# Strassen-Winograd block pairs of weights: the first block sum as A22 + A21, summed by a load and an accumulating DMA, where it was A21 − A22 over a copy of A22 that GpSimd negates

## The chip, the cores and the metric

The kernel runs on one core of one Trainium2 chip. A core has a matrix engine (TensorE, PE in the profile; its weight loads are listed apart as PEld), VectorE (DVE), ScalarE (ACT), GpSimd (POOL) and SyncE (SP, which here only issues DMAs), and 16 DMA engines that move data between the memory of the chip (HBM) and the core's on-chip memory. Matrix products land in PSUM. The metric is the time of one execution on the device, in microseconds (us).

## What is computed

Two layers of a small diffusion transformer over 256 latent tokens and 256 context tokens, width 1024, all in fp32. Each layer has a gated feed-forward network (FFN, hidden width 2816), a mixer, and a second FFN; layer 0 mixes by a short convolution, layer 1 by attention. Cut to what matters here:

```python
def _swiglu(h, w13, w2):
    gte, up = jnp.split(h @ w13, 2, axis=-1)
    return (jax.nn.silu(gte) * up) @ w2

def _short_conv_mixer(h, w_in, k, w_out):
    bgate, cgate, xv = jnp.split(h @ w_in, 3, axis=-1)
    return (bgate * _dwconv3(cgate * xv, k)) @ w_out
```

The FFNs run on latent and context tokens together (512 columns), except the last one, which runs on the latent tokens alone.

## The kernel before

**Tiling.** Activations are held transposed: features on the 128 partitions, tokens along the free dimension. An fp32 product is made of three matmuls: every operand is split into a high and a low part (`split`, L106: ScalarE rounds the high part, L107; VectorE subtracts to get the low part, L108), and `mm3` (L132) adds high·high (L136), high·low (L137) and low·high (L138) in PSUM.

**Block pairs.** Two tiles of 128 output features (gate and up of one hidden tile, for instance) times two halves of the contraction (512 features each) times two halves of the tokens (latent and context) make a 2×2 by 2×2 block product. The class `Pair` (L697 to L787) computes it by the Strassen-Winograd scheme: seven block products of 12 matmuls each (128×128 weights, 256 tokens) where the plain way needs eight. It needs sums of the weight blocks, S1 to S4, and sums of the activation blocks, T1 to T4. The T sums are made once for an input (`Blocks.sums`, L407, and `FirstBlocks.sums`, L443), the S sums for every pair. There are 66 pairs: 56 in the FFNs (first matrix `w13`) and 10 in the convolution mixer (`cw_cx`, `cw_b`). The first tiles of a stage (two, or six in the first FFN) are computed the plain way (`opening`, L789, the first steps of the kernel and L830), while the blocks are still being normalised.

**How one pair gets its weights.** In HBM a pair's weights are one row of 2048 columns for each partition, as four blocks of 512 columns: A21, A11, A22, A12. `Pair.__init__` (L704) fills two raw tiles of 1024 columns, r1 and r2, from a pool of eight such buffers (tag `wr`):

- SP loads r2 = [A22 | A12], 512 KB (`load_raw`, L103).
- SP loads A11 into the right half of r1, 256 KB (L708).
- POOL writes −A22 into the left half of r1 (L710), which needs r2 landed and r1's buffer free.
- POOL issues a DMA that adds A21 from HBM onto it (L713): S1 = A21 − A22.
- A11 and A12 are split for the products that use them as they are (L718).

`sums(0)` then has VectorE turn A11 into S2 = A11 − S1 in place (L732), and r1 as a whole, S1 beside S2, is split in one go (L733, by L107 and L108). `sums(1)` splits A22 into tiles of their own, w4h and w4l: ScalarE makes the high part and its negative (L112, L113), and a DMA issued by POOL adds A22 from HBM again (L114). Then VectorE subtracts S2 from both halves of r2 (L740: S3 = A22 − S2, S4 = A12 − S2), and r2 is split.

**Order of the products.** `head` (A11, A12), `five` (S1·T1, the first to need S1; its matmuls write q and read th, tl), `six` (S2·T2, S4·B22), then `seven` (S3·T3) and `four` (A22·T4) of the pair before. Between them ScalarE copies partial sums out of PSUM (L757, L763, L767) and VectorE adds and multiplies the results (L769, L777, L786).

**What sets the order.** Each engine and each queue runs its instructions in one fixed order and waits on semaphores. That order is laid out when the program is built, by a planner with modelled costs of instructions, except where the code holds it by hand (`manual_schedule`: the first steps and the attention heads) or ties one instruction behind another (`issue_after`). POOL's queue carries, beside L710 and L713, the A22 accumulations (L114) and those that add an FFN's output to x (L567), all in one line. Other users of the `wr` buffers are the second FFN matrices (`w2a`, `w2b`) and the rows of the modulation matrix (`modT`), which VectorE reduces in the gaps (L177). An FFN goes in three parts, each a run of pairs and then a projection by `w2`; the first pairs of the next part are loaded during the projection.

## Time and profile before

| quantity | value |
| --- | --- |
| runs of the kernel | 1545.27, 1545.4, 1546.8 us; median 1545.4 us |
| the profiled execution: its time | 1545.56 us |
| the profiled execution: span from first to last instruction | 1543.8 us |
| busy time PEld, DVE, ACT, POOL | 1423.8, 1299.2, 850.3, 301.3 us |
| granted TensorE clock, whole span | 1.000 |
| moved by DMA | 278.80 MB, mean 181 GB/s; 262.07 MB read from HBM |

The profile is of one execution, so terms are compared with its own span; its time is 1.8 us above its span and 0.16 us above the median of the runs. A line of the timeline reads: start in us from the first instruction, duration in us, engine, line of the code, operation, tile written <- tiles read, shapes, count, and in brackets the idle time of the engine before it with what ended it. A line of the windows reads: stretch, its length, then for each engine its busy time and count of instructions, the granted clock, the mean busy share of the 16 DMA engines, and GB/s.

### The profile page before, as it was taken

How to read it: one execution, taken by the hardware profiler on the slowest of the kernel's cores; microseconds unless marked ns; L12 is line 12 of the kernel's file. 1: busy time of each engine (PE TensorE's matmuls, PEld its weight loads, DVE VectorE, ACT ScalarE, POOL GpSimd, SP SyncE). 2: the span in 40 equal slices, each digit the busy share in tenths (PEclk: the TensorE clock that was granted, in tenths of full speed). 3: DMA queues.
4: the chain of work that ended last, by engine and by line, in shares of the span. 5: the costliest groups of instructions: out<-in, count | busy, mean ns of one | idle time of the engine just before them, and what ended most of it. 6: DMA issues, size and time to landing. Idle time of an engine off the chain costs nothing.

```text
span 1543.8 us, 27341 instructions
## 1 busy us (share of the span) xinstructions
PE 1532.5 (99%) x10594; PEld 1423.8 (92%) x10594; DVE 1299.2 (84%) x1970; ACT 850.3 (55%) x1474; POOL 301.3 (20%) x265
## 2 busy tenths in 40 slices
PE   9999999999999999999999999999999999999999
PEld 6898998999999899999899899989899899998888
DVE  5888788898999999978979889958868788897676
ACT  5644554645665376446456476446456456774553
POOL 0003313402231022042152102142052002300000
PEclk9999999999999999999999999999999999999999
DMA  9568768775356646686796625786697743476562
GB/s 380 198 191 232 161 186 227 170 193 143 76 144 181 201 104 142 216 208 150 209 212 149 213 72 127 222 184 149 212 218 175 257 156 112 150 244 219 169 195 76
DMA packets 97474, 278.80 MB, mean 181 GB/s; under 512 B 11456, under 2 KB 13120, under 8 KB 97344
## 3 DMA queue, kind: packets, MB, share of 16 engines
q1 hardware_dynamic: 69408, 228.10, 45.9%
q0 software_dynamic: 25920, 47.20, 18.3%
q10 hardware_dynamic: 2016, 1.76, 0.4%
q8 instruction: 83, 1.36, 0.4%
q14 instruction: 47, 0.39, 0.1%
HBM read 262.07 MB, written 1.05 MB: 170 GB/s over the span
## 4 chain that ended last, share of the span: by engine, by line
PE 93%; DVE 4%; ACT 1%; DMA 1%; issue 1%; POOL 0%; SPq 0%; DVEq 0%; ACTq 0%; POOLq 0%
PE py L137 9%; PE py L136 9%; PE py L138 9%; PE p L138 8%; PE p L137 8%; PE p L136 8%; PE q L138 6%; PE q L136 6%; PE q L137 6%; PE py L144 2%; PE pu L144 2%; PE pg L144 2%; PE py L146 1%; DVE wl L108 1%; PE pg L146 1%; PE pu L146 1%
## 5 line engine op out<-in xcount | busy, mean ns | idle before, releaser
L107 ACT ACTIVATE wh<-wr 128x1024 fp32r<-128x1024 f32 (+2 forms) x454 | 401.2, 909 | 303.9 <-PE py L137 96.2
L108 DVE TENSOR_TENSOR wl<-wr,wh 128x1024 fp32r<-128x1024 f32 (+2 forms) x454 | 469.8, 1057 | 105.5 <-ACT wh L107 83.8
L177 DVE CUSTOM_DVE_ANT_0 junk<-wr,scbc,first 128x1024 bf16<-128x1024 f32 x209 | 270.4, 1294 | 2.2 <-DMA wr<-in_modT 0.2
L137 PE MATMUL py<-gl,wh 128*128 128x512 f32 (+1 forms) x570 | 213.4, 374 | 0.0
L136 PE MATMUL py<-gh,wh 128*128 128x512 f32 (+1 forms) x570 | 213.4, 374 | 0.0
L138 PE MATMUL py<-gh,wl 128*128 128x512 f32 (+1 forms) x570 | 212.8, 373 | 0.0
L710 POOL TENSOR_SCALAR wr<-wr 128x512 f32<-128x512 f32 x66 | 125.9, 1907 | 423.2 <-DMA wr<-in_w 182.3
L137 PE MATMUL p<-tl,wh 128*128 128x256 f32 x528 | 149.4, 283 | 0.0
L138 PE MATMUL p<-th,wl 128*128 128x256 f32 x528 | 149.4, 283 | 0.0
L136 PE MATMUL p<-th,wh 128*128 128x256 f32 x528 | 149.4, 283 | 0.0
L138 PEld LDWEIGHTS py<-gh,wl 128*128 128x128 f32 x570 | 107.3, 188 | 19.2
L136 PEld LDWEIGHTS py<-gh,wh 128*128 128x128 f32 x570 | 107.4, 188 | 18.3
L137 PEld LDWEIGHTS py<-gl,wh 128*128 128x128 f32 x570 | 107.4, 189 | 18.0
L138 PE MATMUL q<-bh,wl 128*128 128x256 f32 x400 | 113.2, 283 | 0.0
L137 PE MATMUL q<-bl,wh 128*128 128x256 f32 x400 | 113.2, 283 | 0.0
L136 PE MATMUL q<-bh,wh 128*128 128x256 f32 x400 | 113.2, 283 | 0.0
L137 PEld LDWEIGHTS p<-tl,wh 128*128 128x128 f32 x528 | 101.3, 192 | 0.4
L136 PEld LDWEIGHTS p<-th,wh 128*128 128x128 f32 x528 | 101.3, 192 | 0.4
L138 PEld LDWEIGHTS p<-th,wl 128*128 128x128 f32 x528 | 101.3, 192 | 0.0
L114 POOL DMA_DIRECT2D w4l<-in_w x56 | 52.8, 944 | 231.9 <-ACT w4l L113 174.6
L567 POOL DMA_DIRECT2D x<-yg x48 | 45.3, 1008 | 213.5 <-ACT yg L564 172.7
L740 DVE TENSOR_TENSOR wr<-wr,wr 128x1024 f32<-128x1024 f32 x66 | 81.5, 1235 | 1.8 <-ACT w4h L112 0.2
(321 smaller groups left out, 4154.1 us busy)
## 6 DMA issues: line engine op xcount, KB each, us to landing
wr<-in_w SPq DMA_DIRECT2D x120, 512.0 KB, 5.0
wr<-in_modT SPq DMA_DIRECT2D x113, 512.0 KB, 5.1
wr<-in_w2b SPq DMA_DIRECT2D x64, 448.0 KB, 3.9
wr<-in_w2a SPq DMA_DIRECT2D x32, 512.0 KB, 4.6
wr<-in_w SPq DMA_DIRECT2D x56, 256.0 KB, 4.3
wr<-in_w POOLq DMA_DIRECT2D x56, 256.0 KB, 6.0
w4l<-in_w POOLq DMA_DIRECT2D x56, 256.0 KB, 5.6
x<-yg POOLq DMA_DIRECT2D x48, 256.0 KB, 7.8
```

What stands on the lines that cost most here:

```text
L107: nc.scalar.activation(out=hi, in_=src, func=AF.Copy)
L108: return nc.vector.tensor_tensor(out=lo, in0=src, in1=hi.bitcast(F32), op=ALU.subtract)
L114: nc.gpsimd.dma_start(out=lo, in_=src, accum_op=ALU.add)
L136: nc.tensor.matmul(ps, wh, mh, start=first, stop=False, **kw)
L137: nc.tensor.matmul(ps, wh, ml, start=False, stop=False, **kw)
L138: return nc.tensor.matmul(ps, wl, mh, start=False, stop=last, **kw).ins
L144: nc.tensor.matmul(ps, w[0], m[2], start=first and n == 0, stop=False)
L146: nc.tensor.matmul(ps[:, :S], w[1], m[0], start=False, stop=last and n == len(ms) - 1)
L177: nc.vector.tensor_tensor_reduce(out=junk, in0=raw, in1=scbc[:, v, :], scale=0.5 if ch in (2, 8) else 1.0, scalar=modb[:, l, col : col + 1 ...
L567: nc.gpsimd.dma_start(out=x[:, m, :], in_=t, accum_op=ALU.add)
L710: nc.gpsimd.tensor_scalar(out=r1[:, :T2], in0=r2[:, :T2], scalar1=-1.0, scalar2=None, op0=ALU.mult)
L740: tt(out=v(r2), in0=v(r2), in1=s2.unsqueeze(1).to_broadcast([P, 2, T2]), op=ALU.subtract,)
```

## The change

`Pair` and the T sums take the other signs of the scheme: S1 = A22 + A21, S2 = S1 − A11, T3 = B22 − B12, T2 = B22 − T1; S3, S4, T1 and T4 keep their forms. r1 becomes [A11 | A22] by one load of 512 KB, as the two blocks lie side by side in HBM, and POOL's DMA adds A21 onto the right half. POOL's negated copy is gone, A22 is read from HBM twice by plain loads (into r1 and r2), and S2 and S1 swap places in r1.

```diff
             elif n == 1:
-                tt(out=b12, in0=b22, in1=b12, op=ALU.add)
-                tt(out=b22, in0=b22, in1=b11, op=ALU.add)
+                tt(out=b12, in0=b22, in1=b12, op=ALU.subtract)
+                tt(out=b22, in0=b22, in1=b11, op=ALU.subtract)
                 keep("T2", b22)
...
             for q in range(2):
-                tt(out=b(0, 1, q), in0=b(1, 1, q), in1=b(0, 1, q), op=ALU.add)
-                tt(out=b(1, 1, q), in0=b(1, 1, q), in1=b(0, 0, q), op=ALU.add)
+                tt(out=b(0, 1, q), in0=b(1, 1, q), in1=b(0, 1, q), op=ALU.subtract)
+                tt(out=b(1, 1, q), in0=b(1, 1, q), in1=b(0, 0, q), op=ALU.subtract)
                 keep("T2", q, b(1, 1, q))
...
             r2 = load_raw(src[:, 1024:2048])
             r1 = wp.tile([P, 1024], F32, name=nm("wr"), tag="wr", bufs=8)
-            nc.sync.dma_start(r1[:, T2:], src[:, T2:1024])
-
-            nc.gpsimd.tensor_scalar(
-                out=r1[:, :T2], in0=r2[:, :T2], scalar1=-1.0, scalar2=None, op0=ALU.mult
-            )
-            nc.gpsimd.dma_start(out=r1[:, :T2], in_=src[:, :T2], accum_op=ALU.add)
+            nc.sync.dma_start(r1, src[:, T2 : T2 + 1024])
+
+            nc.gpsimd.dma_start(out=r1[:, T2:], in_=src[:, :T2], accum_op=ALU.add)
             self.raw = [r1, r2]
             ts = half()
             for i, key in enumerate(("A11", "A12")):
                 self.w[key] = [t[:, i * T2 : i * T2 + T2] for t in ts]
-                split(*self.w[key], self.raw[i][:, T2:])
+                split(*self.w[key], self.raw[i][:, i * T2 : i * T2 + T2])
...
             r1, r2 = self.raw
-            s1, s2 = r1[:, :T2], r1[:, T2:]
+            s1, s2 = r1[:, T2:], r1[:, :T2]
             tt = nc.vector.tensor_tensor
             if n == 0:
-                tt(out=s2, in0=s2, in1=s1, op=ALU.subtract)
-                self.keep(("S1", "S2"), r1)
+                tt(out=s2, in0=s1, in1=s2, op=ALU.subtract)
+                self.keep(("S2", "S1"), r1)
                 return
```

## The prediction

> **What bounds the kernel now.** I read the page first, then TensorE's waits, then single stretches.

> ```profile
> span 1543.8 us, 27341 instructions
> ...
> PE 1532.5 (99%) x10594; PEld 1423.8 (92%) x10594; DVE 1299.2 (84%) x1970; ACT 850.3 (55%) x1474; POOL 301.3 (20%) x265
> ...
> q1 hardware_dynamic: 69408, 228.10, 45.9%
> ...
> PE 93%; DVE 4%; ACT 1%; DMA 1%; issue 1%; POOL 0%; SPq 0%; DVEq 0%; ACTq 0%; POOLq 0%
> ```

> TensorE is busy 99% of the span and holds 93% of the chain that ended last; POOL, whose work the change takes away, holds 0% of it. A busy TensorE need not be at its full rate, so I looked at the count of matmuls in stretches of pure pair work:

> ```profile
> 800.00:820.00 20.00, 20.00 (x169) 20.00 (x168) 17.74 (x26) 12.68 (x22) 7.49 (x7) 1.00 0.60 129
> 1160.00:1180.00 20.00, 20.00 (x169) 20.00 (x168) 17.52 (x23) 12.65 (x23) 6.62 (x6) 1.00 0.80 182
> 260.00:280.00 20.00, 18.69 (x136) 17.64 (x135) 16.51 (x22) 10.55 (x19) 11.22 (x11) 1.00 0.98 225
> ```

> 169 matmuls in 20 us, 118 ns each, at a DMA share of 0.60 and at 0.80 alike: there TensorE runs at its own pace and neither loads nor POOL slow it. The third row is another kind of place, the start of a part of an FFN, where pairs and projection meet: the 16 DMA engines are full (0.98) and TensorE loses 1.3 us. All its waits between 60 and 1200 us, where all pairs lie:

> ```profile
> PE pg L136 <- ACT bh L391: 1.4, 1, 1.4
> PE q L136 <- ACT gm L763: 1.3, 1, 1.3
> PE p L138 <- DVE wl L108: 0.6, 1, 0.6
> PE pg L137 <- DVE bl L392: 0.2, 1, 0.2
> ```

> These are 3.5 us. That is the most that any relief of the other engines can visibly bring; beyond it only the 118 ns could shrink, and the change takes away no matmul.

> **The change part by part. 1, the signs.** Subtractions take the place of additions and S1 swaps sides with S2. Both operations are there now, at the same shape:

> ```profile
> L769 DVE TENSOR_TENSOR sg<-q,sg 128x512 f32<-128x512 f32 x66 | 45.3, 686 | 4.0 <-PE q L138 1.8 <-ACT wh L107 1.1 <-issue 0.5
> L732 DVE TENSOR_TENSOR wr<-wr 128x512 f32<-128x512 f32 x66 | 45.2, 685 | 9.8 <-DMA wr<-in_w 9.6
> L710 POOL TENSOR_SCALAR wr<-wr 128x512 f32<-128x512 f32 x66 | 125.9, 1907 | 423.2 <-DMA wr<-in_w 182.3 <-DVE wl L108 134.7 <-ACT wh L107 35.4
> ```

> The addition (L769) takes 686 ns, the subtraction (L732) 685: cost 0.

> **2, the negated copy.** 66 copies of 1907 ns leave POOL: 125.9 us. On the chain of POOL that is nothing, as it holds 0%. They may also hold up VectorE while they run. Two places show it:

> ```profile
> 257.76 2.09 POOL L710 TENSOR_SCALAR wr<-wr 128x512 f32<-128x512 f32 x1
> 258.04 1.48 DVE L108 TENSOR_TENSOR wl<-wr,wh 128x512 fp32r<-128x512 f32 x1
> ```
> ```profile
> 407.43 2.36 DVE L108 TENSOR_TENSOR tl<-hr,th 128x1024 fp32r<-128x1024 f32 x2
> 407.61 3.52 POOL L710 TENSOR_SCALAR wr<-wr 128x512 f32<-128x512 f32 x1 [22.03 <-DVE wl L108]
> ```

> At 258 us a subtraction of 128x512 takes 1.48 us beside a copy, where L732 takes 0.69: 0.79 us lost in a copy of 2.09, a share of 0.38, which over 125.9 us would be 48 us of VectorE time. At 407 us it is POOL that loses (3.52 instead of 1.91 us), and two subtractions take 1.18 us each. So VectorE gets back between 0 and 48 us of its 1299.2. TensorE sees of that only what it waits for VectorE, 0.6 + 0.2 us; the 0.6 follows right behind the copy at 407 us, where VectorE wasn't slowed, so I take 0 there and keep −0.8 as the bound. At 258 us VectorE idles soon after (below): 0.

> [...]

> **3, the larger load.** 66 times 256 KB more on SP's queue are 17.3 MB. That queue's 228.10 MB took 45.9% of 1543.8 us, 3.1 us for each MB, so the addition is 54 us of DMA time, 0.81 us in each pair of 9.9 us (84 matmuls of 118 ns); a share of 0.80 becomes 0.88. How much later r1 lands:

> ```profile
> wr<-in_w SPq DMA_DIRECT2D x120, 512.0 KB, 5.0
> ...
> wr<-in_w SPq DMA_DIRECT2D x56, 256.0 KB, 4.3
> ```

> 0.7 us between the medians. At worst, where the engines are full, 262 kB at 225 GB/s are 1.2 us; at best 0, if the bytes go beside the others. I take 0.7 in steady stretches, as the medians come mostly from there, and 1.2 at starts.

> **4, what S1 waits for.** Now L713 follows the copy, which needs r2 landed and r1's buffer free. After, it needs r1's own load landed. A steady pair, with the landing of the load issued at 1154.31 and of the accumulation issued at 1156.84 below it:

> ```profile
> 1154.02 0.87 POOL L114 DMA_DIRECT2D w4l<-in_w  x1 [7.14 <-ACT w4l L113]
> 1154.31 0.33 SPq L708 DMA_DIRECT2D wr<-in_w  x1
> 1154.59 1.84 POOL L710 TENSOR_SCALAR wr<-wr 128x512 f32<-128x512 f32 x1
> 1156.84 0.91 POOL L713 DMA_DIRECT2D wr<-in_w  x1 [0.41 <-POOL wr L710]
> 1167.84 0.68 DVE L732 TENSOR_TENSOR wr<-wr 128x512 f32<-128x512 f32 x1
> 1171.20 0.28 PE L138 MATMUL p<-th,w4l 128*128 128x256 f32 x1
> ```
> ```profile
> DMA to landing us min/median/max: 3.4/3.4/3.4
> ```
> ```profile
> DMA to landing us min/median/max: 6.3/6.3/6.3
> ```

> Now S1 lands at 1156.84 + 6.3 = 1163.1 and VectorE uses it at 1167.84: a lead of 4.7 us. After: 1154.31 + 3.4 + 0.7 for the load, 0.4 for the handover to POOL as in the bracket of L713, so L713 starts at 1158.8 instead of 1156.84 and S1 lands at 1165.1. The lead falls to 2.7 us; cost 0. Waiting behind L713 in POOL's line are accumulations of A22 (L114) and of x. The one issued at 1154.02 is used first at 1171.20, 17 us on; 2 us of delay cost nothing there. Without the lead, VectorE would wait in L732, and everything behind it with it.

> **5, the starts of the parts.** There is no lead:

> ```profile
>   DMA wr<-in_w: 9.6, 6
> ```
> ```profile
> 256.47 0.92 POOL L713 DMA_DIRECT2D wr<-in_w  x1 [0.41 <-POOL wr L710]
> 261.92 0.69 DVE L732 TENSOR_TENSOR wr<-wr 128x512 f32<-128x512 f32 x1 [1.19 <-DMA wr<-in_w]
> 266.07 3.75 DVE L108 TENSOR_TENSOR wl<-wr,wh 128x1024 fp32r<-128x1024 f32 x3
> 267.65 0.28 PE L136 MATMUL q<-th,wh 128*128 128x256 f32 x1
> 270.63 1.06 ACT L107 ACTIVATE wh<-wr 128x1024 fp32r<-128x1024 f32 x1 [1.77 <-PE p L137]
> ```
> ```profile
> 782.28 0.69 DVE L732 TENSOR_TENSOR wr<-wr 128x512 f32<-128x512 f32 x1 [1.68 <-DMA wr<-in_w]
> 784.22 2.83 DVE L108 TENSOR_TENSOR wl<-wr,wh 128x1024 fp32r<-128x1024 f32 x2
> 789.85 0.28 PE L136 MATMUL q<-th,wh 128*128 128x256 f32 x1
> ```
> ```profile
> DMA to landing us min/median/max: 8.4/8.4/8.4
> ```

> In 6 of the 66 pairs VectorE stood at L732 until S1 landed (first row, from the line's own waits), 9.6 us together. In the pair of L713 at 256.47 the load into r1 had been issued at 247.0 and took 8.4 (the last row), to 255.4. After: 255.4 + 1.2 + 0.4 = 257.0 instead of 256.47, so S1 comes 0.5 us later, and up to 1.7 if the accumulation loses another 1.2 in the full queues. The low half of S1 is ready at 266.07 + 3.75/3 = 267.3 and TensorE takes it at 267.65: a lead of 0.3. TensorE's loss there is 0.2 to 1.4 us; I take **0.5**, near the lower end, because removing the copy also removes the 0.79 that VectorE lost at 258. At 782 us the low half is ready at 784.22 + 1.4 = 785.6 and wanted at 789.85: 4.2 us of lead hide such a delay. The loss of 1.3 us at 271 (TensorE waiting for L763) has ScalarE's order as its cause: L763 stands behind the L107 of 270.63, which itself waits for TensorE. The change doesn't touch that: 0.

> **The sum**: 0 + 0 + 0 + 0 + 0.5 = +0.5 us on the profiled execution's 1545.56, 1546.1; that execution lies 0.16 above the median, so **1545.9 us**, with 1544.6 (−0.8) to 1546.8 (+1.4) as this case's own bounds.

> **The rivals. A, slower: S1 comes too late at the starts.** 225 GB/s for 20 us are 4.5 MB; a pair now takes 1.31 MB (512 + 3 x 256 KB), so I estimate three pairs in such a burst: 0.79 MB more, 3.5 us at that rate. If all of it falls ahead of S1, the start at 256 us loses 3.5 − 0.3 = 3.2 us: 1548.6. If the 2.0 us by which L713 moved in the steady pair come on top, it loses 5.2 there, and 5.5 − 4.2 = 1.3 at each of the other five: 11.7, so 1557. It decides from the point where S1 lands over 4.2 us later at a start. For it speaks the share of 0.98; against it, that r1's load had landed (255.4) before L713 began at 256.47, and that the first pair of a burst has only its own bytes ahead of it.

> **B, another order.** The planner lays out every engine's line anew from changed costs. One misplaced instruction costs 1.3 us now (L107 ahead of L763); three more make +3.9, 1549.3, and setting that one right −1.3, 1544.1. No row says which.

> **C, faster: every wait of TensorE in the pairs goes**, VectorE's line being 48 us shorter: 1545.4 − 3.5 = 1541.9. Against it, 2.7 of the 3.5 us are waits for ScalarE.

> **D, POOL wins nothing**: its idle time before L710 (423.2 us) moves to L713. That is inside the forecast, as POOL holds nothing up.

> **How the numbers follow.** About 0.2%, 3.1 us, is what a measurement of this kernel can tell from no change. Forecast with D 0.48, all within it. A 0.24, all slower. B 0.15: 0.10 slower, 0.02 within, 0.03 faster. C 0.13: 0.10 faster, 0.03 within. Together faster 0.13, within 0.53, slower 0.34. The range 1542 to 1554 takes in B, nearly all of C and A but for its upper third; about 0.15 stays outside.

> **What would show it.** Right: 169 matmuls in 20 us of steady pairs, L713 some 4.5 us behind L708, L732 idle for S1 in 6 to 12 pairs with TensorE's waits below 5 us. VectorE's mean for the 128x512 subtractions falls towards 0.69 us. Wrong: TensorE waiting for L108 or L763 at several starts (A), new waits of TensorE far from S1 with the loads in time (B), or the 118 ns of a matmul changed, for which I have no mechanism.

## The result, and the profile after

The changed kernel takes 1552.64 us (median of 6 runs, 1551.38 to 1557.73) where the kernel before takes 1546.05 us beside it (6 runs, 1545.27 to 1547.29): a ratio of 1.0045, 95% interval 1.0035 to 1.0055. It is slower, and 6.6 us by the medians. The time lies in the predicted range, but the likeliest case, no change, did not come about. The profiled execution took 1554.74 us, 2.1 above that median, with a span 9.2 us longer than the one before; so the places below add up to more than the 6.6 us between the medians. Page of the changed kernel: span, busy time, SP's queue (packets, MB, share of 16 engines), and the loads that SP issues into pairs (KB each, median us to landing).

```profile
span 1553.0 us, 27168 instructions
...
PE 1535.8 (99%) x10594; PEld 1425.7 (92%) x10594; DVE 1282.5 (83%) x1970; ACT 849.4 (55%) x1474; POOL 181.5 (12%) x199
...
q1 hardware_dynamic: 69408, 245.40, 48.4%
...
wr<-in_w SPq DMA_DIRECT2D x176, 512.0 KB, 5.1
```

VectorE gained 16.7 us (1299.2 to 1282.5), GpSimd 119.8 us, and TensorE's busy time rose by 3.3 us with as many matmuls. The windows say where this isn't and where it is:

```profile
1180.00:1200.00 20.00, 20.00 (x169) 20.00 (x169) 17.48 (x25) 12.77 (x22) 2.60 (x3) 1.00 0.81 201
260.00:280.00 20.00, 19.17 (x125) 17.24 (x124) 14.93 (x20) 11.02 (x21) 6.09 (x7) 1.00 1.03 248
1140.00:1160.00 20.00, 17.06 (x130) 16.86 (x129) 11.73 (x16) 8.94 (x17) 4.35 (x5) 0.91 0.87 188
```

Steady pairs run as before, 169 matmuls in 20 us. From 1140 to 1160 us, the start of the third FFN's last part, there are 130, where the kernel before has 169, and the granted clock falls to 0.91. TensorE's longest waits between 60 and 1210 us, and VectorE's wait for S1 at S2 (us, times, longest):

```profile
PE q L136 <- ACT gm L760: 3.5, 2, 2.9
PE q L138 <- DVE wl L108: 2.0, 1, 2.0
PE pg L136 <- ACT bh L391: 1.4, 1, 1.4
```
```profile
DVE wr L729 <- DMA wr<-in_w: 32.6, 10, 4.5
```

The first two waits of TensorE are new or longer; VectorE's wait for S1 was 9.6 us in 6 pairs and is 32.6 us in 10.

TensorE runs the same 10594 matmuls in the same order in nearly all of these kernels, so two traces can be paired matmul by matmul. The start of a matmul in one trace less that of its partner in the profile before is the delay so far, and its growth over a stretch is what that stretch costs. For the changed kernel that is 0.6 us before 60 us (no pair is running there), **2.3 at 103 us**, 0.4 around 270, 0.5 around 380, **4.7 at 1141 to 1153 us** and 0.7 in all other places: 9.2.

**The place at 1144 us.** The chain of waits that ended last runs through it (start, us, what; the first row is the load of r2):

```profile
1119.20 10.45 DMA wr<-in_w
...
1133.97 2.30 issue
...
1137.18 1.50 issue
1138.69 7.00 DMA wr<-in_w
...
1145.78 0.70 DVE wr L729
...
1147.61 0.36 ACT gm L760
...
1148.02 0.38 PE q L136
```

GpSimd's own rows of the same stretch (timeline), and the time to landing of three DMAs: r1's load, issued by SP at 1120.20, then GpSimd's of 1128.80 and of 1129.45:

```profile
1128.80 0.88 POOL L710 DMA_DIRECT2D wr<-in_w  x1 [2.49 <-DMA wr<-in_w]
1129.45 1.12 POOL L114 DMA_DIRECT2D w4l<-in_w  x1
1133.11 0.86 POOL L114 DMA_DIRECT2D w4l<-in_w  x1 [2.54 <-ACT wh L107]
1136.29 0.89 POOL L567 DMA_DIRECT2D x<-yg  x1 [2.31 <-issue]
1138.69 0.87 POOL L710 DMA_DIRECT2D wr<-in_w  x1 [1.52 <-DVE wr L737]
```
```profile
DMA to landing us min/median/max: 11.9/11.9/11.9
```
```profile
DMA to landing us min/median/max: 7.2/7.2/7.2
```
```profile
DMA to landing us min/median/max: 8.9/8.9/8.9
```

The raw tile of this pair had landed at 1120.20 + 11.9 = 1132.1, but its accumulation (the last L710) was issued only at 1138.69. In GpSimd's line it stands behind two accumulations of A22 (L114) and one of x (L567); before, it was issued at 1129.34, and the second of these L114 and the L567 came behind it (timeline of the kernel before):

```profile
1129.34 0.91 POOL L713 DMA_DIRECT2D wr<-in_w  x1 [2.52 <-issue]
1131.12 0.89 POOL L114 DMA_DIRECT2D w4l<-in_w  x1 [0.88 <-ACT wh L107]
1132.36 0.87 POOL L567 DMA_DIRECT2D x<-yg  x1 [0.36 <-issue]
```

And those in front were held up: the L567 of 1136.29 starts 0.3 us after the DMA of 1128.80 landed (1128.80 + 7.2 = 1136.0), the L710 of 1138.69 0.3 us after that of 1129.45 (1138.4). Counted over the 180 DMAs that GpSimd issues, never more than two earlier ones are still under way at an issue, before and after the change alike (66 and 67 of the 180 find two). So the third waits here for the first, whether that carries S1, as the DMA of 1128.80, or A22, as that of 1129.45. The bracket of the last row of the changed kernel puts this down to VectorE's L737, which was done at 1138.03; the two stretches of "issue" in the chain are the better reading.

S1 lands at 1138.69 + 7.0 = 1145.7. Before, it landed at 1129.34 + 4.0 = 1133.3. Of these 12.4 us, 4.2 are the delay so far; the other 8.2 are 3.0 from r1's load, 2.2 from the time between its landing and the issue (6.6 us, 4.4 before) and 3.0 from the accumulation itself (7.0 us, 4.0 before). VectorE's S2 (L729) waits for S1, ScalarE's L107 for S2, and the copy L760, which has nothing to do with this S1 (it takes the product S1·T1 of the pair before out of PSUM), is queued behind that L107. TensorE needs L760's result, and stands 2.9 us. Then a second price (windows, the granted clock is the third number from the end):

```profile
1144.00:1148.00 4.00, 1.08 (x10) 0.87 (x8) 2.18 (x3) 1.32 (x2) 0.89 (x1) 1.00 1.09 263
...
1150.00:1152.00 2.00, 2.00 (x11) 2.00 (x11) 1.37 (x2) 0.59 (x1) 0.23 (x1) 0.50 0.77 173
...
1153.00:1154.00 1.00, 1.00 (x10) 1.00 (x10) 0.00 (x0) 0.00 (x1) 0.00 (x0) 1.00 1.02 213
```

The granted clock is 0.50 from 1149.6 to 1153.0, and the matmuls start 213 ns apart instead of 120: 3.4 us in which TensorE starts 16 matmuls, 1.9 us of work at 120 ns each. By the pairing the stop costs 3.2 us and the halved clock 1.5, which is the 4.7.

**The place at 103 us** is the first FFN's second pair. Timeline of the changed kernel:

```profile
87.41 0.33 SPq L708 DMA_DIRECT2D wr<-in_w  x1
...
91.52 0.90 POOL L710 DMA_DIRECT2D wr<-in_w  x1 [6.72 <-DMA wr<-in_w]
...
99.39 0.69 DVE L729 TENSOR_TENSOR wr<-wr 128x512 f32<-128x512 f32 x1 [2.49 <-DMA wr<-in_w]
```
```profile
105.42 0.39 PE L138 MATMUL q<-th,wl 128*128 128x256 f32 x1 [2.02 <-DVE wl L108]
```

The same pair in the kernel before (timeline; the first of the two L108 makes the low half of S1):

```profile
85.96 0.33 SPq L708 DMA_DIRECT2D wr<-in_w  x1
88.25 0.91 POOL L713 DMA_DIRECT2D wr<-in_w  x1 [0.36 <-DMA wr<-in_w]
96.22 0.69 DVE L732 TENSOR_TENSOR wr<-wr 128x512 f32<-128x512 f32 x1
100.98 2.35 DVE L108 TENSOR_TENSOR wl<-wr,wh 128x1024 fp32r<-128x1024 f32 x2
102.41 0.28 PE L136 MATMUL q<-th,wh 128*128 128x256 f32 x1
```

The accumulation starts 4.1 us after the load was issued; before, it started 2.3 us after, as it did not wait for that load. It also takes 7.8 us instead of 5.3, and the load is issued 0.9 us later, so S1 lands 5.1 us later beyond the delay so far (1.8 + 2.4 + 0.9). Before, S1 landed 2.6 us ahead of VectorE's S2, and the low half of S1 was ready 0.2 us ahead of the first matmul of S1·T1. The two leads add up along the chain, to 2.8 us, and 5.1 us are more: VectorE waits 2.5 us, and TensorE stands 2.0 us at the matmul that reads the low half of S1.

### The profile page after: what moved, and what is told of

It is laid out like the page before. It is cut to its first block, busy times and chain, and to the rows that moved or that the text cites. A ratio compares the mean times of both kernels' runs of the same rounds, so it can differ in the third digit from the quotient of the medians.

```text
span 1553.0 us, 27168 instructions
## 1 busy us (share of the span) xinstructions
PE 1535.8 (99%) x10594; PEld 1425.7 (92%) x10594; DVE 1282.5 (83%) x1970; ACT 849.4 (55%) x1474; POOL 181.5 (12%) x199
## 3 DMA queue, kind: packets, MB, share of 16 engines
q1 hardware_dynamic: 69408, 245.40, 48.4%
## 5 line engine op out<-in xcount | busy, mean ns | idle before, releaser
L107 ACT ACTIVATE wh<-wr 128x1024 fp32r<-128x1024 f32 (+2 forms) x454 | 401.2, 909 | 304.2 <-DVE wr L729 86.8
L108 DVE TENSOR_TENSOR wl<-wr,wh 128x1024 fp32r<-128x1024 f32 (+2 forms) x454 | 461.1, 1038 | 107.6 <-ACT wh L107 88.5
L137 PE MATMUL py<-gl,wh 128*128 128x512 f32 (+1 forms) x570 | 213.4, 374 | 0.0
L136 PE MATMUL py<-gh,wh 128*128 128x512 f32 (+1 forms) x570 | 213.4, 374 | 0.0
L138 PE MATMUL py<-gh,wl 128*128 128x512 f32 (+1 forms) x570 | 212.8, 373 | 0.0
L136 PE MATMUL p<-th,wh 128*128 128x256 f32 x528 | 149.6, 283 | 0.3 <-ACT sg L754 0.2
L138 PE MATMUL p<-th,wl 128*128 128x256 f32 x528 | 149.4, 283 | 0.0
L137 PE MATMUL p<-tl,wh 128*128 128x256 f32 x528 | 149.4, 283 | 0.0
L138 PEld LDWEIGHTS py<-gh,wl 128*128 128x128 f32 x570 | 107.3, 188 | 19.1
L136 PEld LDWEIGHTS py<-gh,wh 128*128 128x128 f32 x570 | 107.4, 188 | 18.5
L137 PEld LDWEIGHTS py<-gl,wh 128*128 128x128 f32 x570 | 107.4, 188 | 18.0
L136 PE MATMUL q<-bh,wh 128*128 128x256 f32 x400 | 113.5, 284 | 2.9 <-ACT gm L760 2.9
L138 PE MATMUL q<-bh,wl 128*128 128x256 f32 x400 | 113.4, 283 | 0.0
L137 PE MATMUL q<-bl,wh 128*128 128x256 f32 x400 | 113.3, 283 | 0.0
L136 PEld LDWEIGHTS p<-th,wh 128*128 128x128 f32 x528 | 101.1, 192 | 1.1 <-ACT sg L754 0.7
L137 PEld LDWEIGHTS p<-tl,wh 128*128 128x128 f32 x528 | 101.1, 192 | 0.4
L138 PEld LDWEIGHTS p<-th,wl 128*128 128x128 f32 x528 | 101.1, 192 | 0.0
L114 POOL DMA_DIRECT2D w4l<-in_w x56 | 52.2, 933 | 391.9 <-ACT w4l L113 290.1
L737 DVE TENSOR_TENSOR wr<-wr,wr 128x1024 f32<-128x1024 f32 x66 | 80.6, 1221 | 3.6 <-ACT w4h L112 3.1
L770 ACT ACTIVATE sg<-sg 128x512 f32<-128x512 f32 x56 | 35.3, 630 | 84.5 <-DVE sg L766 84.5
L710 POOL DMA_DIRECT2D wr<-in_w x56 | 49.1, 877 | 265.4 <-DMA wr<-in_w 75.6
## 6 DMA issues: line engine op xcount, KB each, us to landing
wr<-in_w SPq DMA_DIRECT2D x176, 512.0 KB, 5.1
wr<-in_modT SPq DMA_DIRECT2D x113, 512.0 KB, 4.9
wr<-in_w2a SPq DMA_DIRECT2D x32, 512.0 KB, 4.6
w4l<-in_w POOLq DMA_DIRECT2D x56, 256.0 KB, 5.7
wr<-in_w POOLq DMA_DIRECT2D x56, 256.0 KB, 6.1
x<-yg POOLq DMA_DIRECT2D x48, 256.0 KB, 7.8
pm<-in_mod SPq DMA_DIRECT2D x16, 512.0 KB, 9.9
```

Of the source, the lines that this page charges most:

```text
L107: nc.scalar.activation(out=hi, in_=src, func=AF.Copy)
L108: return nc.vector.tensor_tensor(out=lo, in0=src, in1=hi.bitcast(F32), op=ALU.subtract)
L114: nc.gpsimd.dma_start(out=lo, in_=src, accum_op=ALU.add)
L136: nc.tensor.matmul(ps, wh, mh, start=first, stop=False, **kw)
L137: nc.tensor.matmul(ps, wh, ml, start=False, stop=False, **kw)
L138: return nc.tensor.matmul(ps, wl, mh, start=False, stop=last, **kw).ins
```

## The experiments

All kernels are compared with the kernel before on the same chip. The last columns are the growth of the delay against the first profile of before (us, by pairing the matmuls as above).

| kernel | median us | ratio, 95% interval | to 60 us | at 103 | around 270 | around 380 | at 893 | at 1144 | elsewhere |
| --- | --- | --- | --- | --- | --- | --- | --- | --- | --- |
| the changed kernel | 1552.64 | 1.0045 (1.0035 to 1.0055) | 0.6 | 2.3 | 0.4 | 0.5 | 0.0 | 4.7 | 0.7 |
| the same, on another occasion | 1553.34 | 1.0038 (1.0025 to 1.0050) | 1.5 | 1.8 | 1.0 | 0.4 | 0.0 | 2.5 | 0.5 |
| 1 new signs, copy kept | 1547.35 | 1.0001 (0.9992 to 1.0010) | 0.6 | 0.0 | 0.9 | 0.0 | 0.0 | 0.0 | 0.3 |
| 2 r1 loaded ahead of r2 | 1548.44 | 1.0009 (1.0000 to 1.0017) | 0.9 | 0.0 | −0.7 | 1.1 | 3.6 | 0.0 | −1.1 |
| 3 copy kept, late accumulation | 1548.54 | 1.0005 (0.9996 to 1.0014) | 0.8 | 1.8 | 0.6 | 0.0 | 0.0 | 0.0 | 0.3 |
| 4 larger descriptor scratch | 1549.93 | 1.0015 (1.0007 to 1.0024) | 1.0 | 1.8 | 2.2 | 0.4 | 0.0 | 0.6 | 0.4 |
| 5 both 2 and 4 | 1548.35 | 1.0007 (0.9998 to 1.0015) | 0.4 | 0.0 | −0.7 | 0.1 | 3.2 | 0.0 | −0.4 |
| 6 kernel before, larger scratch | 1547.01 | 0.9998 (0.9989 to 1.0007) | 1.0 | 0.0 | 0.6 | 0.0 | 0.0 | 0.0 | −0.1 |
| 7 r1 in two loads, A22 first | 1550.18 | 1.0018 (1.0009 to 1.0027) | 0.8 | 0.0 | −1.6 | 0.8 | 4.6 | 0.0 | −1.1 |
| 8 as 7, one pair put back | 1545.47 | 0.9991 (0.9982 to 1.0000) | 0.8 | 0.0 | −1.6 | 1.1 | 0.0 | 0.0 | −1.4 |
| 9 copy kept, a further load | 1551.76 | 1.0030 (1.0018 to 1.0041) | | | | | | | |
| 10 GpSimd adds, no DMA for S1 | 1560.01 | 1.0081 (1.0067 to 1.0094) | | | | | | | |
| 11 VectorE adds, no DMA for S1 | 1570.65 | 1.0154 (1.0137 to 1.0171) | | | | | | | |

The first of these columns differs by up to 1 us between executions whatever the edit (0.6 and 1.5 for the changed kernel), and the one around 270 by 0.6 or more (0.6 in experiment 6, 0.9 in experiment 1), so only larger growth at one place is read from the table, not the sum. Experiments 9 to 11 lose in many places and are left out of it.

How late S1 lands, less the delay so far, tells the loss at both places in all these kernels. At 103 us it lands 5.1 us later than before in the changed kernel and 4.6 to 4.7 on the other occasion and in experiments 3 and 4, where 1.8 to 2.3 us are lost; it lands 0.9 later or earlier than before in the others, where nothing is lost. At 1144 us it lands 8.2, 7.4 and 5.6 us later in the changed kernel, on the other occasion and in experiment 4, where 4.7, 2.5 and 0.6 are lost; it lands at most 4.0 later in the others, where nothing is lost.

**1. The signs alone.** The new signs and sides, with GpSimd's copy of A22 (now without the minus) and the load of 256 KB as before. Against the changed kernel:

```diff
-            nc.sync.dma_start(r1, src[:, T2 : T2 + 1024])
+            nc.sync.dma_start(r1[:, :T2], src[:, T2:1024])
+            nc.gpsimd.tensor_scalar(
+                out=r1[:, T2:], in0=r2[:, :T2], scalar1=1.0, scalar2=None, op0=ALU.mult
+            )
```

> The new signs alone: A11 is loaded alone (256 KB) as before, and GpSimd copies A22 from r2 into r1 with a factor of +1 instead of -1; loads, copies and accumulations are those of the kernel before. Theory (the loss comes from S1 landing late at the starts of the parts): 1545 to 1547 us, VectorE idle at the S2 subtraction some 10 us in 6 pairs. Rival (the signs or the swapped sides of S1 and S2 cost something): 1549 us or more.

1547.35 us, a ratio of 1.0001, VectorE's wait for S1 10.3 us in 6 pairs, and no growth of the delay at 103 or 1144 us. The signs and the swapped sides cost nothing: the loss belongs to the larger load, the missing copy and what S1 now waits for.

**2. The same bytes, S1's load first.** The changed kernel, with the load of r1 issued ahead of that of r2:

```diff
+            r1 = load_raw(src[:, T2 : T2 + 1024])
             r2 = load_raw(src[:, 1024:2048])
-            r1 = wp.tile([P, 1024], F32, name=nm("wr"), tag="wr", bufs=8)
-            nc.sync.dma_start(r1, src[:, T2 : T2 + 1024])
```

> The changed kernel with r1's load of 512 KB issued ahead of r2's; the bytes stay, the accumulation waits for the first load instead of the second. Theory dependency (S1 is late because its accumulation waits for the second load): 1545.5 to 1548.5 us, VectorE's idle time at the S2 subtraction back from 32.6 us to 10 to 18. Rival bytes (the 17.3 MB more keep the full DMA engines from delivering in time, whatever the order): 1551 to 1554 us, idle time 25 us or more.

1548.44 us, 1.0009. Both places are gone from the table; VectorE waits 9.3 us for S1 in 5 pairs. In exchange there is a stop of 2.4 us at 893 us, where TensorE waits for VectorE's sum of squares:

```profile
PE ss L269 <- DVE acc L262: 3.5, 2, 2.4
```

The further 17.3 MB are still all there, so most of the 0.45% is not their transport as such. The edit moves more than the load, though: the planner lays out GpSimd's line anew, and at 1144 us S1's accumulation stands ahead of the second L114, as in the kernel before.

**3. The dependency alone.** Experiment 1, with one column of A11 read by GpSimd ahead of the accumulation. S1 then waits for r1's load of 256 KB, without further bytes:

```diff
-            nc.gpsimd.dma_start(out=r1[:, T2:], in_=src[:, :T2], accum_op=ALU.add)
+            seen = const.tile([P, 1], F32, name=nm("seen"), tag="seen")
+            at = nc.gpsimd.tensor_scalar(
+                out=seen, in0=r1[:, :1], scalar1=1.0, scalar2=None, op0=ALU.mult
+            ).ins
+            with tc.issue_after(at):
+                nc.gpsimd.dma_start(out=r1[:, T2:], in_=src[:, :T2], accum_op=ALU.add)
```

> The dependency without the bytes: the kernel of the signs alone, with a one-column GpSimd instruction between copy and accumulation that reads A11 in r1, so that the accumulation starts only when r1's own load (256 KB) has landed; no byte more than before. It leaves the output unchanged. Theory dependency: 1549 to 1553 us, idle time of VectorE at the S2 subtraction 20 us or more. Rival bytes: 1545.5 to 1547.5 us.

1548.54 us, 1.0005: between the two expectations, with VectorE's wait for S1 at 19.0 us. This alone brings back the place at 103 us, with 1.8 us, and nothing at 1144 us:

```profile
PE q L138 <- DVE wl L108: 1.8, 2, 1.5
```

So at 103 us the dependency is enough, while 1144 us needs something more. Neither the bytes nor the dependency makes the whole loss alone.

**4. The limit on GpSimd's queue.** The changed kernel, with twice the memory for the descriptors of GpSimd's DMAs:

```diff
-    nc = _bacc.Bacc("TRN2", target_bir_lowering=False, num_devices=1, dynamic_dma_scratch_size=1024)
+    nc = _bacc.Bacc("TRN2", target_bir_lowering=False, num_devices=1, dynamic_dma_scratch_size=2048)
```

> The changed kernel with twice the memory for the descriptors of GpSimd's DMAs. In both traces no accumulation was issued with more than two earlier ones still under way, and GpSimd stood for up to 3.5 us before an issue until the third one back had landed. Theory ring (that limit holds S1's accumulation up behind those of A22 and x): 1547 to 1550 us, more than two under way at an issue. Rival (dependency or bytes, the limit is no cause): 1552 to 1554 us.

1549.93 us, 1.0015. Every engine's order is that of the changed kernel, but now up to five earlier DMAs are under way when GpSimd issues one. Its rows at the place of 1144 us:

```profile
1133.02 0.86 POOL L114 DMA_DIRECT2D w4l<-in_w  x1 [1.88 <-ACT w4l L113]
1133.75 1.05 POOL L567 DMA_DIRECT2D x<-yg  x1
1134.39 1.31 POOL L710 DMA_DIRECT2D wr<-in_w  x1
```

The three follow each other at 0.7 us instead of waiting for landings, and S1's accumulation is issued at 1134.39, 0.6 us behind the landing of its load at 1133.8 (6.6 us behind it in the changed kernel). The accumulation itself then takes 10.0 us instead of 7.0, so S1 lands 5.6 us later than before instead of 8.2. The place costs 0.6 us instead of 4.7. At 103 us, where GpSimd's line is empty, nothing changes (1.8 us). In exchange TensorE stops 2.0 us at 270 us for the low half of S1, with 3.4 us at half clock behind it:

```profile
272.85 0.58 PE L138 MATMUL q<-th,wl 128*128 128x256 f32 x1 [2.04 <-DVE wl L108]
```

**The changed kernel again, 5. both remedies, and 6. the limit without the change.** These three ran beside each other. 5 is experiment 2 with the larger scratch, 6 the kernel before with it; the edits are those shown.

> The changed kernel once more, beside the next three on one chip. Theory now held (S1 of a part's second pair comes too late, since its accumulation starts only when a load twice as large has landed in full DMA engines, and POOL has at most two earlier DMAs under way): 1.0035 to 1.0055 of the kernel before, as in its first runs, with a stop of TensorE of 2 us or more at about 103 or about 1144 us. Rival (the loss belongs to single executions or to one chip): below 1.0020 here.

> The changed kernel with the load of r1 issued ahead of that of r2 and with the larger descriptor scratch, both at once. Alone they brought the ratio from 1.0045 to 1.0009 and to 1.0015. Theory (both act on the same lateness of S1): together no better than the kernel before, 0.9997 to 1.0010, DVE's wait for S1 at S2 below 15 us where it was 32.6 in the changed kernel. Rival (two separate losses, each worth its own 0.30 to 0.36%): the gains add to 0.66%, a ratio of 0.998. Second rival (the order that the planner finds with r1 first is itself worse at one place, as the wait of 2.4 us at 896 us suggests): above 1.0010.

> The kernel before, with the larger descriptor scratch only. Theory (the limit of DMAs under way on POOL's queue costs time only where S1 hangs on a late load): no difference, 0.9994 to 1.0006. Rival (the limit costs the kernel before as much as it costs the changed one): 0.9970, as the scratch alone brought the changed kernel from 1.0045 to 1.0015.

The loss repeats (1.0038), at the same two places. This profile has a stop of 2.2 us at 1144 us, and the clock stays at full: 2.5 us are lost there instead of 4.7. Both remedies together bring 1.0007, no better than 2 alone within the intervals, so they act on the same lateness and their gains do not add; what is left is a stop of 2.0 us at 893 us, as in 2. The kernel before gains nothing from a larger scratch (0.9998): the limit on GpSimd's queue costs time only once S1 hangs on a late load.

**7. S1 on the first and smallest load.** r1 in two halves: A22 first, then r2, then A11.

```diff
-            r2 = load_raw(src[:, 1024:2048])
             r1 = wp.tile([P, 1024], F32, name=nm("wr"), tag="wr", bufs=8)
-            nc.sync.dma_start(r1, src[:, T2 : T2 + 1024])
+            nc.sync.dma_start(r1[:, T2:], src[:, 1024:1536])
+            r2 = load_raw(src[:, 1024:2048])
+            nc.sync.dma_start(r1[:, :T2], src[:, T2:1024])
```

> The changed kernel with r1 loaded in two halves of 256 KB: A22 into its right half ahead of r2, A11 into its left half behind r2. Same bytes and the same accumulation, but S1 hangs on the first and smallest load of the pair. Theory (the loss is S1's wait for a late load at the second pairs of a part, in full DMA engines): DVE's wait for S1 at S2 as in the kernel before or below (under 10 us), 0.9995 to 1.0010. Rival (17.3 MB more in full DMA engines cost time wherever S1 hangs): 1.0025 or more.

1550.18 us, 1.0018: between the two expectations. VectorE's wait for S1 is lower than in any kernel so far (4.4 us in 2 pairs), and 1.6 us are even won around 270 us. But one place costs 4.6 us. Timeline of this kernel there:

```profile
891.55 0.63 ACT L112 ACTIVATE w4h<-wr 128x512 fp32r<-128x512 f32 x1 [4.58 <-DMA wr<-in_w]
892.08 0.61 ACT L260 ACTIVATE sq<-x 128x512 f32<-128x512 f32 x1
```
```profile
896.08 0.61 PE L269 MATMUL ss<-ones,acc 128*128 128x1 f32 x4 [3.39 <-DVE acc L262]
```

What is late here is r2, not S1: it is now second in SP's line, and waited there for a free `wr` buffer until 884.64. ScalarE's L112 needs r2, the squares (L260) are queued behind L112, VectorE adds them up (L262), and TensorE stands 3.4 us for the sum, with the clock at half behind it (the granted clock is 0.69 from 896 to 901 us and 0.93 from 901 to 903; the matmuls of 128x256 start 213 ns apart).

**8. One pair put back.** Experiment 7, with r2 first again in the second pair of the third FFN, and in no other (a third argument of `Pair`, true for this pair alone, puts the load of r2 first):

```diff
-                        pr = Pair(a["w13"][l, b, i0 + i], h)
+                        pr = Pair(a["w13"][l, b, i0 + i], h, (l, b, i0 + i) == (1, 0, 3))
```

> The kernel with r1 in two loads, the first of them ahead of r2 (1.0018), with one of the 66 pairs put back to r2 first: the second pair of the third FFN, where TensorE stood 3.4 us for VectorE's sum of squares at 893 us, because ScalarE's squares were queued behind L112, which waited 4.6 us for r2. Theory (with S1 on a small early load nothing of the change costs time, and what is left of that kernel's loss is this one wait and the lower clock behind it, 4.5 us): the stop at 893 us goes, TensorE's waits for L269 fall below 1.5 us, and the ratio becomes 0.9980 to 1.0000. Rival (17.3 MB more cost 0.1 to 0.2% wherever they are put): 1.0010 or more, though the stop goes.

1545.47 us, 0.9991 (0.9982 to 1.0000). The stop is gone, and the waits for the sum and for S1 are small:

```profile
PE ss L269 <- DVE acc L262: 1.1, 1, 1.1
```
```profile
DVE wr L733 <- DMA wr<-in_w: 3.8, 2, 2.1
```

The rival (the further bytes cost 0.1 to 0.2% wherever they are put) falls: this kernel moves the same 245.40 MB on SP's queue. It is the fastest version tried, at most 0.2% ahead of the kernel before and perhaps level with it.

**9. A further load that nothing waits for.** Experiment 1 with a further load of 140 KB for each pair, right behind r1's, into a tile that nothing reads:

```diff
+            more = wp.tile([P, 280], F32, name=nm("more"), tag="more", bufs=2)
+            nc.sync.dma_start(more, src[:, 1024:1304])
```

> The new signs with GpSimd's copy kept (the first of the experiments), and a further load of 140 KB for each pair, right behind r1's, into a tile that nothing reads: 55% of the change's further bytes (9.5 MB) with S1 hanging on the same loads as in the kernel before. Theory (bytes alone cost little): 0.9995 to 1.0010, TensorE's stops at 103 and 1144 us absent. Rival (the bytes are the loss): 55% of 0.45%, 1.0020 to 1.0030.

1551.76 us, 1.0030, as the rival had it. It does not decide, though. The further tile has two buffers, and SP itself stood waiting for them, with all later loads behind it (SP's waits):

```profile
SPq L710 <- DMA more<-in_w: 70.8, 34, 7.2
```

The delay grows by 8.5 us between 119 and 195 us, where the changed kernel loses nothing, and by nothing at 1144 us. It measures a held-up queue more than bytes. Its matmuls also start at other spacings than in the kernel before (128x256 at 118 ns instead of 120, 128x512 at about 233 instead of 227), for a reason that is not known. Experiment 8 answers the question better.

**10 and 11. No accumulating DMA for S1.** r1 = [A21 | A11] by one load of 512 KB, and an engine adds A22 from r2: GpSimd in 10, VectorE (its line below) in 11. S1 and S2 swap sides with it.

```diff
-            r1 = wp.tile([P, 1024], F32, name=nm("wr"), tag="wr", bufs=8)
-            nc.sync.dma_start(r1, src[:, T2 : T2 + 1024])
-
-            nc.gpsimd.dma_start(out=r1[:, T2:], in_=src[:, :T2], accum_op=ALU.add)
+            r1 = load_raw(src[:, :1024])
+            nc.gpsimd.tensor_tensor(out=r1[:, :T2], in0=r1[:, :T2], in1=r2[:, :T2], op=ALU.add)
...
+                tt(out=s1, in0=s1, in1=r2[:, :T2], op=ALU.add)
```

> The changed kernel without the accumulating DMA of S1: r1 = [A21 | A11] comes by one load of 512 KB, and GpSimd adds A22 from r2 onto its left half (66 additions of 128x512 where the kernel before had 66 copies). As many bytes as the kernel before, one DMA fewer in each pair. Theory (the loss is the second of two DMAs in a row): S1 is ready one addition behind the loads, DVE waits at S2 below 10 us, 0.9990 to 1.0005 of the kernel before. Rival (GpSimd's addition, with two inputs, takes and costs more than the copy of 1.9 us did): POOL's addition takes 3 us or more, DVE's busy time rises above the 1299 us of the kernel before, ratio 1.0005 to 1.0030.

> S1 without an accumulating DMA, as in the run in which GpSimd added A22 onto A21 (1.0081), but VectorE adds: 66 additions of 128x512 of 0.69 us, 45 us more of VectorE's time and no addition on GpSimd. There VectorE's busy time had risen by 52 us over the changed kernel. Theory (TensorE lost there because VectorE came late, whatever made it late): VectorE's busy time about 1328 us, ratio 1.005 to 1.010. Rival (the two-input addition of GpSimd did harm of another kind): 1.0000 to 1.0030.

10 gives 1560.01 us, 1.0081, slower than either theory had it. Its additions take 1.63 us, less than the 1.91 of the copies, but VectorE's busy time is 1334.3 us, 51.8 more than in the changed kernel. Timeline of 10:

```profile
808.60 1.31 POOL L708 TENSOR_TENSOR wr<-wr,wr 128x512 f32<-128x512 f32 x1 [8.34 <-DMA wr<-in_w]
808.68 1.79 DVE L727 TENSOR_TENSOR wr<-wr 128x512 f32<-128x512 f32 x1
```

S2 takes 1.79 us instead of 0.69. It loses 1.10 of the 1.23 us that the addition had left to run, nearly all of them.

11 gives 1570.65 us, 1.0154, beyond its expectation, though VectorE is busier by less than in 10 (1318.6 us). So VectorE's busy time does not explain the loss; where the addition stands in its line is the likelier cause (VectorE's waits):

```profile
DVE wr L726 <- DMA wr<-in_w: 55.8, 20, 6.1
```

VectorE itself waits 20 times for a load, with everything behind it. In 10 GpSimd, which has spare time, does this waiting (377.4 us of idle time ahead of its additions, 197.6 of them for these loads).

## Why the prediction was right or wrong

The sum gave +0.5 us, with 1544.6 to 1546.8 as its bounds; the medians differ by 6.6 us. The range held because the rivals widened it, not because the sum was near. Of the signs, the 169 matmuls, the start of S1's accumulation and the 10 pairs came as written; TensorE's waits between 60 and 1210 us are 8.8 us, not below 5. The 118 ns of a matmul are 120 by the starts of neighbours: 169 counts those that lie across an edge of the window.

- **Step 1, the signs: right.** Cost 0 (experiment 1).
- **Step 2, the copy: right.** VectorE's relief had bounds of 0 and 48 us; it is 16.7 us, 13% of the copies' 125.9 us, and the mean of the 128x512 subtractions into wl fell from 707 to 687 ns. TensorE's waits of 0.6 and 0.2 us for VectorE are still there, so it gained nothing from this.
- **Step 3, the larger load: right where it was read, too small at the starts.** In steady pairs a stretch still has 169 matmuls. At 1120 us, however, a load of r1 took 11.9 us, where that pair's load of 256 KB took 8.9 us before (1116.0 to 1124.9). I had allowed 1.2 us. The accumulation of S1, which I had allowed another 1.2 us there, took 3.0 us longer (7.0 instead of 4.0), and 2.4 longer at 103 us.
- **Step 4, the lead in steady pairs: right.** I expected L713's successor 4.5 us behind the load of r1, with 2.7 us of lead left. In the pair loaded at 1163.17 it starts 4.8 us behind, and 2.0 us are left.
- **Step 5, the starts of the parts: this step failed.** At 256 us it held: S1 lands 0.8 us later beyond the delay so far, for a forecast of 0.5, and TensorE loses 0.4 at S1·T1 (0.6 in the second profile), for a forecast of 0.5. That is no evidence for the larger load, though: in experiments 1 and 6, which load 256 KB as before, S1 lands 1.1 and 1.0 us later and TensorE loses 0.7 and 0.5 there. And I priced that place alone and took the others as covered, by the lead of 4.2 us that I had read at 782 us and a lateness of S1 of 0.5 to 1.7 us; at 103 and 1144 us it was 5.1 and 8.2. Three things were missed. First, I looked for endangered pairs in VectorE's waits at L732. The pair at 103 us had no such wait before, but only 2.8 us of lead in all. Second, I took S1 as issued as soon as its load had landed. GpSimd's line was laid out anew, with L114 and L567 ahead of S1, and its queue had no more than two earlier DMAs under way at any issue: 6.6 us between landing and issue at 1144 us. Experiment 4 takes away the limit, and 4.1 of the 4.7 us go (1.9 of the 2.5 in the second profile). Third, I counted the lead only up to TensorE's use of S1. At 1144 us TensorE stops earlier than that, for a copy (L760) queued behind an L107 that waits for S2; when it reaches S1·T1 after the stop, S1 has been ready for 4.4 us.
- **Rival A (S1 too late at the starts, 1548.6 to 1557) came true**, with a median inside its span. Its price was reached in another way: not six starts losing a little, but two of them losing 2 to 5 us, one by the dependency (experiment 3) and one by GpSimd's line. Of the latter 1.5 us were the halved clock in the first profile, which no term held, and nothing in the second.
- **Rival B (another order)** had a share in it: TensorE's and SP's orders are unchanged, but GpSimd's is not, and one L107 with its L108 stands later in ScalarE's and VectorE's (at 1131.6 and 1132.9 us). The 1.3 us lost at 271 us behind L107, which I had called untouched by the change, are 0.6 in the changed kernel and gone in experiments 7 and 8, although L107 still stands ahead of the copy. Whether S1's earlier landing there does that, or the new order of the other lines, is not shown.
- **Rival C (faster by VectorE's relief)** did not come about: two of TensorE's four waits were for ScalarE, as argued, and the relief was a third of its bound.

What stays open: why the planner put L114 and L567 ahead of S1 in GpSimd's line, and how much of the loss at 1144 us that order makes by itself. A kernel with the changed loads in their order and the old order of GpSimd's line was not tried. In experiment 3 the second L114 stands ahead of S1 too (issued at 1134.59 and 1135.86 us); S1 lands 4.0 us later there, and nothing is lost. Why S1's accumulation takes 7.0 and 10.0 us at 1144 us (changed kernel, experiment 4) where it took 4.0 before, and 7.8 at 103 us where it took 5.3, is open as well.

## What to carry to other kernels

When a step is moved from an engine to a DMA, add up the leads of every pair or tile along the chain from the landing to the engine that bounds the kernel, not only of those that already wait, and compare with how late the landing can become: at 103 us 2.6 + 0.2 us of lead met 5.1 us. The order of a queue mattered more here than its bytes: with the operand that others hang on in the first and smallest load, 17.3 MB more cost nothing measurable in sum (1.1 us lost around 380, 1.6 won around 270), and second in line they cost 0.4%. In these traces an instruction that waited for a load made what was queued behind it wait too, and TensorE with that: 2.9 us by L760 at 1144 us, 3.4 by L260 in experiment 7. So look at what stands behind such an instruction, and put such waits on the engine that has the least queued behind them (here GpSimd rather than VectorE, 1.0081 against 1.0154).
